# The end of a decoder trunk: sums of squares on TensorE, the last residual's place, and whole rows in the output transfers

## The chip, the cores and the metric

The kernel runs on one core of a Trainium2 chip. The metric is the device time of one execution in microseconds (us). The core has five engines that run side by side, each in its own instruction order: TensorE (PE, matrix products into PSUM), VectorE (DVE), ScalarE (ACT), GpSimd (POOL) and SyncE (SP), which issues most DMA transfers. They wait for one another through semaphores.

## The reference

One inference step of a trunk of two layers over 512 prompt tokens and 8 x 8 sample tokens, in float32, model width 1024. What matters here is the end: the feed-forward block of the second layer, its gated residual, and the final norm.

```python
D_MODEL = 1024; D_FF = 2816; EPS = 1e-6
def rms_norm(x, g):
    y = x * lax.rsqrt(jnp.mean(x * x, axis=-1, keepdims=True) + EPS)
    return y * g
def swiglu(h, w_in, w_out):
    gate, up = jnp.split(h @ w_in, 2, axis=-1)
    return (jax.nn.silu(gate) * up) @ w_out
def trunk(...):
    for l in range(DEPTH):
        ...   # layer 0: recurrent block; layer 1: sliding-window attention
        h = modulate(rms_norm(x, norm_g[l, 1]), sh2, sc2)
        x = x + g2[:, None, :] * swiglu(h, ffn_w_in[l], ffn_w_out[l])
        ...
    y = rms_norm(x, final_g)
```

## The kernel before

The tokens are worked on in two halves, h = 0 and h = 1, of 288 columns each: 256 prompt tokens and 32 sample tokens. The stream x[h] lies transposed in SBUF, as eight chunks c = 0 to 7 of 128 channels by 288 tokens; x_64 and x_65 are the two halves in the listings below. A float32 product is made of three float32r products of split operands, so a product of `K` blocks is 3 K matmuls of 128x288 columns (rows `mm<-sl,wh`).

The last stage of the feed-forward block (`out`, with the last group of hidden blocks) makes for each chunk m a product of 12 matmuls into a PSUM bank. `residual` then adds it to x: VectorE adds the prompt part (x<-mm,mods,x), makes the sample part in a buffer (ta<-mm,mods), and GpSimd adds it (x<-x,ta); for the very last chunk, 7, VectorE does that add too. `square` lets ScalarE square the finished chunk into a buffer ta and VectorE add it to the sum acc (acc_69 and acc_70 for the two halves); chunk 7 is not added there. `final_chunk` transposes the chunk on TensorE (mm<-ident,x: two of 128 columns and one of the 32 sample columns), and VectorE multiplies it by the gain into the output tiles (h<-mm,h; h_15729 in half 1): three tiles yt[h][0..2] of 128, 128 and 32 tokens by 1024 channels.

`final_norm`, when chunk 7 is done, squares it, sums over channels by products with a column of ones (mm<-small,acc and mm<-small,ta: the squares stand as weights, the ones are the moving column, one product for each of the three token groups in TOK), turns the sums into mean plus EPS on VectorE (tst<-mm), raises them to the power -1/2 on GpSimd (tst<-tst,small), scales the left 512 channels of each output tile on VectorE and the right 512 on ScalarE (h<-h,tst), and sends each half-tile to memory on SyncE's DMA queue.

Nothing of this is put on the engines as it is written. Every operation is recorded with an estimated cost, and a list scheduler (`schedule`) then fixes each engine's order; a recorded operation's priority is its place in the program, and `early(n)` moves everything inside it n places forward. In the trace every operation therefore has the one line of the recorder, L447, and is told apart by the names of its tiles.

Of the kernel before, what the change touches and what calls it, by code (L numbers as in the profile page):

```python
# [15 lines left out]
AF = mybir.ActivationFunctionType  # L16
ALU = mybir.AluOpType
AX = mybir.AxisListType

P = 128  # L20
D = 1024
KC = D // P
# [4 lines left out]
HP = 256  # L27
HC = 288
CW = 300
XW = 303  # L30
EPS = 1e-6
# [28 lines left out]
SH1, SC1, G1, SH2, SC2, G2 = range(6)  # L60
KVSH, KVSC = 6, 7
L1 = 8
# [411 lines left out]
def trunk_kernel(ctx, tc, a):  # L474
    nc = tc.nc
    rec = Recorder(a["shadow"])
    V, S, G, T, Q = (Engine(rec, n, o) for n, o in (("DVE", nc.vector), ("ACT", nc.scalar), ("POOL", nc.gpsimd), ("PE", nc.tensor), ("SP", nc.sync)))
# [5 lines left out]
    def const(shape, name, dt=F32):  # L483
        return cp.tile(shape, dt, tag=name, name=name)
# [3 lines left out]
    def ps(pool=pmm, tag="mm"):  # L488
        cnt[0] += 1
        return rec.tile(pool, tag, NMM if tag == "mm" else (8 - NMM), RMM if tag == "mm" else 1, [P, 512], F32, f"{tag}{cnt[0]}")  # L490

    def aux():
        return ps()

    x = [const([P, KC, HC], f"x{h}") for h in range(2)]
# [5 lines left out]
    ta = Slots(rec, cp, "ta", SLOT, NTA)  # L501
# [4 lines left out]
    ones, mhalf = small[:, 0:1], small[:, 4:8]  # L506
    mods = const([P, 14, KC, 9], "mods")
    acc = [const([P, HC], f"acc{h}") for h in range(2)]
    rstd = acc
    tst = [const([P, 6], f"tst{h}") for h in range(2)]  # L510
# [21 lines left out]
    @contextmanager  # L532
    def early(n):

        rec.bias -= n
        yield
        rec.bias += n
# [67 lines left out]
    pt = aux()  # L605
# [166 lines left out]
    def mp(g, c):  # L772
        return mods[:, g, c, 0:1]

    def msam(g, c, h):
        return mods[:, g, c, 1 + 4 * h : 5 + 4 * h].unsqueeze(2).to_broadcast([P, 4, NT])

    def v48(t):
        return t.rearrange("p (b t) -> p b t", b=4)


    def square(h, c):
        if c == 0:
            S.activation(acc[h][:], x[h][:, c, :], AF.Square)
        else:
            s = ta()
            S.activation(s.f[:, 0:HC], x[h][:, c, :], AF.Square)
            V.tensor_tensor(acc[h][:], acc[h][:], s.f[:, 0:HC], ALU.add)
            s.done()

    TOK = [slice(0, P), slice(P, 2 * P), slice(2 * P, HC)]

    def stats(h):
        pt = aux()
        st = tst[h][:, 0:3]
        for t, ts in enumerate(TOK):
            T.matmul(pt[0 : ts.stop - ts.start, t : t + 1], acc[h][:, ts], ones, start=True, stop=True)
# [4 lines left out]
    def spread(h, r0=0):  # L802
# [3 lines left out]
        o = aux()  # L806
        for t, ts in enumerate(TOK):
            r = slice(r0, r0 + 32) if t == 2 else ALL
# [152 lines left out]
    def drop(u):  # L961
        u.left -= 1
        if u.left == 0:
            u.hi.done()
            u.lo.done()
            nhi[0] -= 1
# [15 lines left out]
    def product(o, u, ops, first=True, last=True, col=0):  # L982
        n = u.kc * P // u.width
        hi, lo = u.hi.r, u.lo.r
        for k in range(n):
            xh, xl = ops[k]
            ks = slice(k * u.width + col, k * u.width + col + P)
            T.matmul(o, hi[:, ks], xh, start=(first and k == 0), stop=False)
            T.matmul(o, hi[:, ks], xl, start=False, stop=False)
            T.matmul(o, lo[:, ks], xh, start=False, stop=(last and k == n - 1))  # L990
# [17 lines left out]
    def residual(h, o, c, g, last):  # L1008
        xp, xs = x[h][:, c, 0:HP], v48(x[h][:, c, HP:HC])
        V.scalar_tensor_tensor(xp, o[:, 0:HP], mp(g, c), xp, ALU.mult, ALU.add)  # L1010
        t = ta()
        V.tensor_tensor(v48(t.f[:, 0:32]), v48(o[:, HP:HC]), msam(g, c, h), ALU.mult)
        (V if g == L1 + G2 and c == KC - 1 else G).tensor_tensor(xs, xs, v48(t.f[:, 0:32]), ALU.add)
        t.done()
        if last and (g != L1 + G2 or c < KC - 1):
            square(h, c)


# [123 lines left out]
    for i, w in enumerate(seq_):  # L1142
        c = int(w[1:])
# [4 lines left out]
        else:  # L1148
            first, last = ug[0] not in units, not any(v[0] == "g" for v in seq_[i + 1 :])
# [14 lines left out]
    for m in range(KC):  # L1164
# [3 lines left out]
            lambda h, o, m=m: residual(h, o, m, G1, True),  # L1168
# [8 lines left out]
    def ffn(l, g, after):  # L1177
# [18 lines left out]
        for f in range(PLAIN):  # L1196
            for w, ev in ((0, evac_gate), (1, evac_up(f))):
                c = 2 * f + w
# [78 lines left out]
        def pump(want=lambda: True):  # L1277
            while todo and (whs.live + todo[0][0] <= 2 * NHI):
                todo.popleft()[1]()
            assert want()  # L1280
            load_more()
# [69 lines left out]
        def out(k, m, h):  # L1351
            f0, us = outs[k]
            n, u = GROUPS[k], us[m]
            pump(lambda: u.hi is not None)
            o = ps()
            product(o[:, 0:HC], u, [(mid[h][f][0].r[:, 0:HC], mid[h][f][1].r[:, 0:HC]) for f in range(f0, f0 + n)], col=P * (m % 2) if u.width > P else 0)
            last = k == len(GROUPS) - 1
            residual(h, o, m, g, last)
            if last and l == 1:
                final_chunk(h, m)  # L1360
            drop(u)
            pump()
            if m == KC - 1:
                for f in range(f0, f0 + n):
                    for s_ in mid[h][f]:
                        s_.done()
                if last:
                    after(h)
# [404 lines left out]
    for w in ATT.split():  # L1773
        h, n = "AB".index(w[-1]), int(w[1:-1] or 0)
# [10 lines left out]
    yt = [None, None]  # L1785
# [14 lines left out]

    def final_norm(h):

        w = ta()
        S.activation(w.f[:, 0:HC], x[h][:, KC - 1, :], AF.Square)
        pt = [aux()[0 : ts.stop - ts.start, 0:1] for ts in TOK]
        st, rs = tst[h][:, 0:3], tst[h][:, 3:6]
        for i in range(2):
            for o, ts in zip(pt, TOK):
                T.matmul(o, (acc[h], w.f)[i][:, ts], ones, start=i == 0, stop=i == 1)
        w.done()  # L1810
        for t in range(3):
            n = P if t < 2 else 32
            V.tensor_scalar(st[0:n, t : t + 1], pt[t], 1.0 / D, EPS, ALU.mult, ALU.add)
            G.tensor_tensor(rs[0:n, t : t + 1], st[0:n, t : t + 1], mhalf[0:n, 0:1], ALU.pow)
            for i in range(2):
                cs = slice(512 * i, 512 * i + 512)
                y = yt[h][t][0:n, cs]
                if i:
                    S.activation(y, y, AF.Copy, scale=rs[0:n, t : t + 1])
                else:  # L1820
                    V.tensor_scalar(y, y, rs[0:n, t : t + 1], None, ALU.mult)
                if t < 2:
                    Q.dma_start(a["y_prompt"][0, h * HP + t * P : h * HP + (t + 1) * P, cs], y)
                else:
                    Q.dma_start(a["y_sample"][4 * h : 4 * h + 4].rearrange("b t d -> (b t) d")[:, cs], y)

    ffn1 = ffn(1, L1 + G2, final_norm)


# [172 lines left out]
```

## Time and profile before

| what | value |
|---|---|
| median of 3 runs | 1262.38 us (1261.91 to 1264.16) |
| profiled execution | 1263.01 us, its span 1261.2 us |
| TensorE busy | 1237.8 us, 98% of the span |
| VectorE, ScalarE, GpSimd busy | 920.3 us (73%), 663.1 us (53%), 252.7 us (20%) |
| share of the chain that ended last | TensorE 86%, VectorE 6%, ScalarE 4%, DMA 2% |
| output transfers of y | 8 of 256 KB, 4 of 64 KB |

The span runs from the first to the last instruction, and the execution's time lies 1.8 us above it. Busy shares are means over the whole span; the chain is followed back from the last instruction to what released it, step by step.

### The profile page before, as it was taken

The numbers are of one execution on the slowest core, as the hardware profiler recorded it, in microseconds if no ns is written. First come the engines' busy times: TensorE is split into PE (matmuls) and PEld (weight loads), VectorE is DVE, ScalarE is ACT, GpSimd is POOL, SyncE is SP. The second block draws the span as 40 slices with busy tenths as digits, with TensorE's granted clock in tenths as the row PEclk, the third lists the DMA queues.
The fourth block names the chain that finished last, engine by engine and source line by source line (L and its number), as shares of the span: only waits on it lengthen the run. The fifth ranks groups of instructions, "written<-read, shape, count | busy, mean of one in ns | idle before, by whom it ended". The sixth has DMA issues, their size and how long they took to land.

```text
span 1261.2 us, 25276 instructions
## 1 busy us (share of the span) xinstructions
PE 1237.8 (98%) x9532; PEld 1166.9 (93%) x9532; DVE 920.3 (73%) x2283; ACT 663.1 (53%) x1498; POOL 252.7 (20%) x542
## 2 busy tenths in 40 slices
PE   7999999999999999999999999999999999999997
PEld 5798999899899899989998997999999999999997
DVE  6998784795577468656778887558957865875776
ACT  4788973764255335514567678538523542552442
POOL 3456351101100010011024335100011011001011
PEclk8999999999999999999999999999999999999999
DMA  9955554535456655464513220332342232332322
GB/s 306 318 179 188 188 177 151 170 86 171 140 152 191 185 167 184 156 194 137 167 33 75 68 60 27 111 97 97 85 133 68 84 110 76 90 100 80 100 69 76
DMA packets 219755, 165.38 MB, mean 131 GB/s; under 512 B 23629, under 2 KB 204841, under 8 KB 219602
## 3 DMA queue, kind: packets, MB, share of 16 engines
q1 hardware_dynamic: 219186, 163.45, 43.0%
q8 instruction: 75, 1.23, 0.4%
q0 software_dynamic: 448, 0.32, 0.1%
q14 instruction: 46, 0.38, 0.1%
HBM read 160.85 MB, written 4.87 MB: 131 GB/s over the span
## 4 chain that ended last, share of the span: by engine, by line
PE 86%; DVE 6%; ACT 4%; DMA 2%; POOL 1%; issue 1%; SPq 0%; ACTq 0%; DVEq 0%
PE mm L447 82%; PE ada L447 4%; DVE wh L447 1%; DVE ta L447 1%; ACT tb L447 1%; DVE sl L447 1%; ACT ta L447 1%; DVE tb L447 1%; ACT h L447 1%; DMA raw<-in_rnn_w_in_dram 1%; ACT wh L447 1%; POOL h L447 1%; DMA reg<-in_ada_w_dram 1%; ACT sl L447 1%; DMA reg<-in_x_prompt_dram 1%
## 5 line engine op out<-in xcount | busy, mean ns | idle before, releaser
L447 PE MATMUL mm<-h,wh 128*128 128x288 f32 x4128 | 596.2, 298 | 3.8 <-ACT h L447 1.8
L447 PEld LDWEIGHTS mm<-h,wh 128*128 128x128 f32 x4128 | 560.5, 188 | 23.2 <-issue 11.3
L447 PE MATMUL mm<-sl,wh 128*128 128x288 f32 x3218 | 460.6, 296 | 0.4 <-ACT sl L447 0.3
L447 ACT CAST wh<-raw 128x512 fp32r<-128x512 f32 (+2 forms) x380 | 269.1, 721 | 345.7 <-PE mm L447 208.9
L447 PEld LDWEIGHTS mm<-sl,wh 128*128 128x128 f32 x3218 | 436.6, 188 | 9.0 <-issue 5.9
L447 DVE TENSOR_TENSOR wh<-raw,wh 128x512 fp32r<-128x512 f32 (+2 forms) x380 | 310.2, 828 | 59.3 <-ACT wh L447 57.0
L447 DVE SCALAR_TENSOR_TENSOR x<-mm,mods,x 128x256 f32<-128x256 f32 x160 | 77.0, 482 | 136.1 <-PE mm L447 136.0
L447 POOL TENSOR_TENSOR td<-td,td 128x288 f32<-128x288 f32 x38 | 35.5, 934 | 475.8 <-ACT td L447 467.7
L447 POOL TENSOR_TENSOR x<-x,ta 128x32 f32<-128x32 f32 x152 | 55.3, 364 | 331.1 <-DVE ta L447 325.9
L447 PE MATMUL mm<-tb,wh 128*128 128x288 f32 (+1 forms) x488 | 88.5, 296 | 0.4 <-ACT td L447 0.4
L447 PEld LDWEIGHTS mm<-tb,wh 128*128 128x128 f32 x488 | 72.4, 188 | 1.9 <-DVE sl L447 0.8
L447 ACT COPY td<-mm 128x288 f32<-128x288 f32 (+2 forms) x140 | 49.0, 364 | 37.7 <-DVE mm L447 18.0
L447 DVE TENSOR_TENSOR raw<-raw,raw 128x512 f32<-128x512 f32 x76 | 61.4, 808 | 0.9
L447 PE MATMUL mm<-ta,wh 128*128 128x288 f32 (+1 forms) x254 | 56.1, 298 | 0.0
L447 ACT ACTIVATE ta<-x 128x288 f32<-128x288 f32 x56 | 24.8, 444 | 55.6 <-POOL x L447 52.4
L447 DVE TENSOR_TENSOR raw<-raw 128x512 f32<-128x512 f32 x76 | 52.2, 688 | 1.1
L447 DVE TENSOR_TENSOR td<-mm,td 128x288 f32<-128x288 f32 x76 | 34.5, 454 | 23.4 <-PE mm L447 23.3
L447 PE MATMUL ada<-reg,cz 128*32 128x512 f32 (+1 forms) x448 | 49.5, 553 | 0.0
L447 PEld LDWEIGHTS mm<-ta,wh 128*128 128x128 f32 x254 | 41.7, 188 | 1.8 <-ACT wh L447 0.8
L447 ACT ACTIVATE ta<-ta,stat 128x128 f32<-128x128 f32 (+2 forms) x72 | 32.3, 471 | 18.5 <-DVE stat L447 17.7
L447 DVE TENSOR_TENSOR acc<-acc,ta 128x288 f32<-128x288 f32 x54 | 25.1, 464 | 12.4 <-ACT ta L447 12.4
L447 ACT CAST sl<-ta 128x288 fp32r<-128x288 f32 x54 | 23.0, 431 | 18.5 <-DVE ta L447 18.5
(202 smaller groups left out, 1197.9 us busy)
## 6 DMA issues: line engine op xcount, KB each, us to landing
raw<-in_ffn_w_in_dram SPq DMA_DIRECT2D x88, 512.0 KB
reg<-in_ada_w_dram SPq DMA_DIRECT2D x80, 512.0 KB
raw<-in_ffn_w_out_dram SPq DMA_DIRECT2D x48, 384.0 KB
raw<-in_rnn_w_in_dram SPq DMA_DIRECT2D x16, 512.0 KB
reg<-in_kv_ada_w_dram SPq DMA_DIRECT2D x16, 512.0 KB
wh<-in_ada_w_dram SPq DMA_DIRECT2D x24, 256.0 KB
raw<-in_rnn_w_out_dram SPq DMA_DIRECT2D x8, 512.0 KB
raw<-in_ffn_w_out_dram SPq DMA_DIRECT2D x8, 512.0 KB
```

Source lines behind the costliest of these rows:

```text
L447: self.rec.add(eng, lambda: getattr(obj, name)(*map(real, args), **{k: real(v) for k, v in kw.items()}), cost, outs, ins, func, lat, port, ...
```

## The change

The change has three parts. The square of chunk 6 is no longer added to acc on VectorE: it is kept in its buffer (`late_square`) and summed by three more products with ones, into the same PSUM column as acc and the square of chunk 7. All products with ones of a half now go to one PSUM bank, in three columns, so that one VectorE instruction makes the statistic of both 128-token groups and the powers are two GpSimd instructions of one and two columns instead of three. The residual of chunk 7 and the sums are recorded 60 places earlier. And each output tile is sent in one transfer of rows of 1024 channels, instead of two of 512.

```diff
         V.tensor_tensor(v48(t.f[:, 0:32]), v48(o[:, HP:HC]), msam(g, c, h), ALU.mult)
         (V if g == L1 + G2 and c == KC - 1 else G).tensor_tensor(xs, xs, v48(t.f[:, 0:32]), ALU.add)
         t.done()
-        if last and (g != L1 + G2 or c < KC - 1):
+        if last and g == L1 + G2 and c == KC - 2:
+            late_square[h] = s = ta()
+            S.activation(s.f[:, 0:HC], x[h][:, c, :], AF.Square)
+        elif last and (g != L1 + G2 or c < KC - 1):
             square(h, c)
...
-            residual(h, o, m, g, last)
+            with early(60 if last and l == 1 and m == KC - 1 else 0):
+                residual(h, o, m, g, last)
...
-        w = ta()
-        S.activation(w.f[:, 0:HC], x[h][:, KC - 1, :], AF.Square)
-        pt = [aux()[0 : ts.stop - ts.start, 0:1] for ts in TOK]
-        st, rs = tst[h][:, 0:3], tst[h][:, 3:6]
-        for i in range(2):
-            for o, ts in zip(pt, TOK):
-                T.matmul(o, (acc[h], w.f)[i][:, ts], ones, start=i == 0, stop=i == 1)
-        w.done()
+        with early(60):
+            w = ta()
+            S.activation(w.f[:, 0:HC], x[h][:, KC - 1, :], AF.Square)
+            pt = aux()
+            st, rs = tst[h][:, 0:3], tst[h][:, 3:6]
+            sums = (acc[h], late_square[h].f, w.f)
+            for i, y in enumerate(sums):
+                for t, ts in enumerate(TOK):
+                    T.matmul(pt[0 : ts.stop - ts.start, t : t + 1], y[:, ts], ones, start=i + t == 0, stop=i == 2, skip_group_check=True)
+            late_square[h].done()
+            w.done()
+            V.tensor_scalar(st[:, 0:2], pt[:, 0:2], 1.0 / D, EPS, ALU.mult, ALU.add)
+            G.tensor_tensor(rs[:, 0:1], st[:, 0:1], mhalf[:, 0:1], ALU.pow)
+            V.tensor_scalar(st[0:32, 2:3], pt[0:32, 2:3], 1.0 / D, EPS, ALU.mult, ALU.add)
+            G.tensor_tensor(rs[:, 1:3], st[:, 1:3], mhalf[:, 1:3], ALU.pow)
         for t in range(3):
             n = P if t < 2 else 32
-            V.tensor_scalar(st[0:n, t : t + 1], pt[t], 1.0 / D, EPS, ALU.mult, ALU.add)
-            G.tensor_tensor(rs[0:n, t : t + 1], st[0:n, t : t + 1], mhalf[0:n, 0:1], ALU.pow)
             for i in range(2):
-                cs = slice(512 * i, 512 * i + 512)
-                y = yt[h][t][0:n, cs]
+                y = yt[h][t][0:n, 512 * i : 512 * i + 512]
                 if i:
                     S.activation(y, y, AF.Copy, scale=rs[0:n, t : t + 1])
                 else:
                     V.tensor_scalar(y, y, rs[0:n, t : t + 1], None, ALU.mult)
-                if t < 2:
-                    Q.dma_start(a["y_prompt"][0, h * HP + t * P : h * HP + (t + 1) * P, cs], y)
-                else:
-                    Q.dma_start(a["y_sample"][4 * h : 4 * h + 4].rearrange("b t d -> (b t) d")[:, cs], y)
+            y = yt[h][t][0:n, :]
+            if t < 2:
+                Q.dma_start(a["y_prompt"][0, h * HP + t * P : h * HP + (t + 1) * P, :], y)
+            else:
+                Q.dma_start(a["y_sample"][4 * h : 4 * h + 4].rearrange("b t d -> (b t) d"), y)
```

What the scheduler makes of it is seen in three places. TensorE at the end of half 1, before: the last matmul of the last product (mm_16161), then the transposes of chunk 6 (mm_16181) and chunk 7 (mm_16192) and the products with ones.

```order
L447 MATMUL mm_16161<-sl_15749,wh_15717 128x288
L447 MATMUL mm_16181<-ident,x_65 128x128 [waits DVE_49]
L447 MATMUL mm_16181<-ident,x_65 128x128
L447 MATMUL mm_16181<-ident,x_65 32x128 [waits Pool_49]
L447 MATMUL mm_16192<-ident,x_65 128x128 [waits DVE_49]
L447 MATMUL mm_16192<-ident,x_65 128x128
L447 MATMUL mm_16198<-small,acc_70 128x1 [waits DVE_49,PE_49]
L447 MATMUL mm_16201<-small,acc_70 128x1
L447 MATMUL mm_16205<-small,acc_70 32x1 [waits PE_49]
L447 MATMUL mm_16192<-ident,x_65 32x128 [waits DVE_49]
L447 MATMUL mm_16198<-small,ta_16203 128x1 [waits Activation_49]
```

The same place after: the last product is mm_16153, the transposes of chunk 6 are mm_16168, and ta_16175 is the late square.

```order
L447 MATMUL mm_16168<-ident,x_65 128x128 [waits DVE_49]
L447 MATMUL mm_16168<-ident,x_65 128x128
L447 MATMUL mm_16153<-sl_15649,wh_15701 128x288
L447 MATMUL mm_16153<-sl_15661,wh_15701 128x288
L447 MATMUL mm_16177<-small,acc_70 128x1 [waits DVE_49]
L447 MATMUL mm_16177<-small,acc_70 128x1
L447 MATMUL mm_16177<-small,acc_70 32x1
L447 MATMUL mm_16177<-small,ta_16175 128x1 [waits Activation_49]
L447 MATMUL mm_16177<-small,ta_16175 128x1
L447 MATMUL mm_16177<-small,ta_16175 32x1
L447 MATMUL mm_16168<-ident,x_65 32x128 [waits Pool_49]
L447 MATMUL mm_16153<-sl_15649,wh_15717 128x288
```

The transposes of chunk 6 and six products with ones now stand inside the last product, which ends with four matmuls behind them (the first is the last row shown); behind it come the transposes of chunk 7 and the three products with ones of its square.

VectorE in the same stretch, before, from the last product's residual on.

```order
L447 SCALAR_TENSOR_TENSOR x_65<-mm_16161,mods,x_65 128x256 [waits PE_49]
L447 TENSOR_TENSOR ta_16189<-mm_16161,mods 128x32 [waits Pool_49]
L447 TENSOR_TENSOR h_15729<-mm_16181,h_15729 128x128 [waits PE_49]
L447 TENSOR_TENSOR acc_70<-acc_70,ta_16186 128x288 [waits Activation_49]
L447 TENSOR_TENSOR h_15729<-mm_16181,h_15729 128x128
L447 TENSOR_TENSOR h_15729<-mm_16181,h_15729 32x128
L447 TENSOR_TENSOR x_65<-x_65,ta_16189 128x32 [waits DVE_49]
```

After, from the output products of chunk 6 on.

```order
L447 TENSOR_TENSOR h_15729<-mm_16168,h_15729 128x128 [waits PE_49]
L447 TENSOR_TENSOR h_15729<-mm_16168,h_15729 128x128
L447 TENSOR_TENSOR h_15729<-mm_16168,h_15729 32x128
L447 SCALAR_TENSOR_TENSOR x_65<-mm_16153,mods,x_65 128x256 [waits PE_49]
L447 TENSOR_TENSOR ta_16194<-mm_16153,mods 128x32
L447 TENSOR_TENSOR x_65<-x_65,ta_16194 128x32 [waits DVE_49]
```

The add of squares is gone, the output products of chunk 6 stand ahead of the last residual, and its three instructions follow one another.

SyncE's queue at its end, after: the three output tiles of half 0 (h_15697, the two prompt tiles in one row) and the three of half 1. Before, each half had six rows of 512 columns here, each waiting for one engine's half-tile.

```order
L447 DMA out_y_prompt_dram<-h_15697 128x1024 [waits DVE_49,Activation_49] x2
L447 DMA out_y_sample_dram<-h_15697 32x1024 [waits DMAHW5_49,DVE_49,Activation_49]
L447 DMA out_y_prompt_dram<-h_15729 128x1024 [waits DMAHW6_49,DVE_49,Activation_49]
L447 DMA out_y_prompt_dram<-h_15729 128x1024 [waits DMAHW7_49,DVE_49,Activation_49]
L447 DMA out_y_sample_dram<-h_15729 32x1024 [waits DMAHW0_49,DVE_49,Activation_49]
```

Each transfer now waits for VectorE and ScalarE both.

More of the change, by code (lines that the diff above doesn't have):

```diff
@@ L789, in square @@
             s.done()
+    late_square = [None, None]
     TOK = [slice(0, P), slice(P, 2 * P), slice(2 * P, HC)]
```

## The prediction

> **What bounds the kernel now.** I read the page first: TensorE is busy for 98% of the span, so anything put into its stream ahead of the last product is paid for unless it lies in a gap. Then I read the chain of waits of the last 82 us. It runs on TensorE alone until 1251.18 us and then through a tail of 10 us in which no product is left.
>
> ```profile
> 1179.96 71.22 PE mm L447 x545
> ...
> 1251.20 0.48 DVE x L447
> ...
> 1254.29 0.56 POOL tst L447
> ...
> 1254.88 1.33 ACT h L447 x2
> 1256.21 0.61 ACTq L1998
> ```
>
> Next came the timelines of the single engines. VectorE's rows of the tail (start, length, operation, idle time ahead of it) show that between the last residual (x<-mm,mods,x) and the last add of samples (x<-x,ta, 1252.66) lie an accumulation of squares and the output products of chunk 6 (h<-mm,h). The first two rows are the same pair of operations in the first half, where nothing lies between.
>
> ```profile
> 1235.90 0.17 DVE L447 TENSOR_TENSOR ta<-mm,mods 128x32 f32<-128x32 f32 x1
> 1236.10 0.19 DVE L447 TENSOR_TENSOR x<-x,ta 128x32 f32<-128x32 f32 x1
> ...
> 1251.20 0.48 DVE L447 SCALAR_TENSOR_TENSOR x<-mm,mods,x 128x256 f32<-128x256 f32 x1 [0.27 <-PE mm L447]
> 1251.60 0.18 DVE L447 TENSOR_TENSOR ta<-mm,mods 128x32 f32<-128x32 f32 x1
> 1251.70 0.28 DVE L447 TENSOR_TENSOR h<-mm,h 128x128 f32<-128x128 f32 x1
> 1251.90 0.45 DVE L447 TENSOR_TENSOR acc<-acc,ta 128x288 f32<-128x288 f32 x1
> 1252.26 0.47 DVE L447 TENSOR_TENSOR h<-mm,h 128x128 f32<-128x128 f32 x2
> 1252.66 0.17 DVE L447 TENSOR_TENSOR x<-x,ta 128x32 f32<-128x32 f32 x1
> 1253.48 0.67 DVE L447 TENSOR_TENSOR h<-mm,h 128x128 f32<-128x128 f32 x3 [0.65 <-PE mm L447]
> 1254.08 0.28 DVE L447 TENSOR_SCALAR tst<-mm 128x1 f32<-128x1 f32 x3
> 1254.88 1.58 DVE L447 TENSOR_SCALAR h<-h,tst 128x512 f32<-128x512 f32 x3 [0.51 <-POOL tst L447]
> ```
>
> TensorE's rows, at the end of the first half and at the very end. A product with ones (mm<-small) is two instructions in the trace.
>
> ```profile
> 1235.27 0.38 PE L447 MATMUL mm<-sl,wh 128*128 128x288 f32 x1
> 1235.48 0.56 PE L447 MATMUL mm<-small,acc 128*128 128x1 f32 x4
> 1235.91 0.51 PE L447 MATMUL mm<-sl,wh 128*128 128x288 f32 x2
> 1236.35 0.22 PE L447 MATMUL mm<-small,acc 128*32 128x1 f32 x2
> 1236.50 0.40 PE L447 MATMUL mm<-sl,wh 128*128 128x288 f32 x1
> 1236.74 0.27 PE L447 MATMUL mm<-ident,x 128*32 128x128 f32 x1
> 1236.76 0.64 PE L447 MATMUL mm<-sl,wh 128*128 128x288 f32 x3
> 1237.24 0.65 PE L447 MATMUL mm<-small,ta 128*128 128x1 f32 x6
> 1237.82 0.93 PE L447 MATMUL mm<-sl,wh 128*128 128x288 f32 x5
> 1238.59 0.38 PE L447 MATMUL mm<-ident,x 128*128 128x128 f32 x2
> ...
> 1249.20 1.96 PE L447 MATMUL mm<-sl,wh 128*128 128x288 f32 x13
> 1251.00 1.18 PE L447 MATMUL mm<-ident,x 128*128 128x128 f32 x5
> 1252.49 0.73 PE L447 MATMUL mm<-small,acc 128*128 128x1 f32 x6 [0.32 <-DVE acc L447]
> 1253.15 0.28 PE L447 MATMUL mm<-ident,x 128*32 128x128 f32 x1
> 1253.42 0.76 PE L447 MATMUL mm<-small,ta 128*128 128x1 f32 x6
> ```
>
> ScalarE, GpSimd and the DMA queue of SyncE at the end, then the outputs' transfers in slices of 0.2 us (last two numbers: share of the DMA engines, GB/s).
>
> ```profile
> 1252.92 0.44 ACT L447 ACTIVATE ta<-x 128x288 f32<-128x288 f32 x1 [1.19 <-DVE x L447]
> 1254.88 1.95 ACT L447 ACTIVATE h<-h,tst 128x512 f32<-128x512 f32 x3 [1.51 <-POOL tst L447]
> 1255.39 0.35 SPq L447 DMA_DIRECT2D out_y_prompt_dram<-h  x1
> 1257.30 1.16 SPq L447 DMA_DIRECT2D out_y_sample_dram<-h  x2
> 1256.20:1256.40 0.20, 0.00 (x0) 0.00 (x0) 0.20 (x1) 0.20 (x2) 0.00 (x0) 0.50 0.73 266
> 1258.40:1258.60 0.20, 0.00 (x0) 0.00 (x0) 0.00 (x0) 0.00 (x0) 0.00 (x0) 0.50 1.00 379
> 1259.40:1259.60 0.20, 0.00 (x0) 0.00 (x0) 0.00 (x0) 0.00 (x0) 0.00 (x0) 0.50 0.63 154
> ```
>
> The engines are full from 1256.2 to about 1259.5: once begun, the six transfers end when their bytes are through, and the span ends 1.7 us later, at 1261.2.
>
> **The change part by part.**
>
> *Products with ones.* Each half gains three (the square of chunk 6 goes through them instead of the VectorE add). In half 1 the order also moves all six for acc and chunk 6, and the three transposes of chunk 6, from behind the last product to inside it; the products are the same. The matmul step is (1251.00 - 1249.20) / 13 = 0.138 us. A set of three products with ones takes 1237.82 - 1237.24 = 0.58, and the five matmuls behind it 0.77 instead of 0.69, so 0.66 with the switch back. The split set of the first half costs more: from 1235.27 to 1237.24 there are 1.97 us with seven matmuls (0.97) and a 32-row transpose; 0.9 is left. From 1237.82 to 1251.00 there are 84 matmuls (11.59) and six sets of transposes: 1.59 / 6 = 0.26 a set.
>
> First half: three unbroken sets, 3 x 0.66 = 1.98, against 0.9 + 0.66 = 1.56: +0.42. Second half, ahead of the end of the last product: 2 x 0.66 + 0.26 = +1.58. TensorE shows no idle time in this stretch, so the last product ends 2.0 us later. Bounds: 0, if they fell into gaps; 3.2, if every set cost the 0.9 of the split one (3 x 0.9 - 1.56 + 2 x 0.9 + 0.26). I take 2.0, from the unbroken set, because the order now shows unbroken sets.
>
> [...]
>
> *Waits this adds.* The ones of the late square wait for ScalarE; behind them on TensorE stand a transpose and the last four matmuls. Behind the wait of a scaling on GpSimd in half 0 stands the residual's sample part of half 1's chunk 0, which TensorE needs only ten matmuls (1.4 us) into a later product. I cost both at nothing, and come back to them as a rival. The DMA of the first half's outputs is covered by more than 10 us of products.
>
> *The residual ahead.* In the order the last residual still stands behind the three output products of chunk 6. They start 1253.48 - 1253.15 = 0.33 after their last transpose and hold VectorE for 0.60, together 0.93; that transpose stands four matmuls from the end, and those end for VectorE after 4 x 0.138 + (1251.20 - 1251.00) = 0.75. So the residual starts 0.18 late: +0.15 with rounding. Bounds 0 and 0.6.
>
> *From the residual to the first scaling.* Before: 1254.88 - 1251.20 = 3.68. After, from the residual's start: ta at 0.40, the add 0.20 behind it at 0.60 (as at 1236.10) and over at 0.79; square 0.09 later (1252.83 to 1252.92), over at 1.32; ones at 1.38, over at 2.14; the 128x2 statistic at 2.18, 0.13 long (now it waits for all three products); GpSimd 0.08 later, 0.56 long, to 2.95; scaling at 2.98. Gain 0.70: the add of samples comes 0.86 earlier, since the add of squares (0.36) and the output products of chunk 6 (0.20 + 0.40) no longer stand ahead of it, and 0.16 goes back to the wait for all three ones. The output products of chunk 7, 1.19 to 1.86 by the same steps, are done before the ones. Bounds of the gain 0.5 and 0.9.
>
> *Output.* The second power now has two columns; 128x1 takes 0.56 and nothing in the tail has two, so between 0.56 and twice that; it is wanted 0.62 after the first scaling and starts 0.5 ahead of it, so at 0.6 it is on time and at 1.1 it delays tile 1 alone, behind 1.4 us of tile 0's bytes. A transfer of a whole tile must wait for ScalarE's half. Two of ScalarE's scalings take 1.33 us (the chain) and three 1.95, so the step is 0.62 and the first ends 0.71 behind its start; with 0.05 to the issue that is 0.76, instead of 1255.39 - 1254.88 = 0.51 for VectorE's half: +0.25. Three issues fewer gain nothing, since the bytes, 288 rows of 4 KB, are the same and fill the engines without a gap. Rows of 4 KB instead of 2 KB are in no store of this trace; if the last 0.6 us ran at 379 GB/s, 0.2 would be saved, and 0.2 the other way is as far as I go.
>
> Sum: +2.0 + 0.15 - 0.70 + 0.25 = **+1.7 us**. The profiled execution took 1263.01 us for a span of 1261.2; 1264.7 on it. The median of the runs, 1262.38, lies 0.63 below that execution, so I predict **1264.1**, 0.13% more. A measurement of this kernel can tell about 0.2%, 2.5 us, from no change: the forecast is no change that can be told.
>
> **The rivals.**
> *TensorE waits for the late squares (slower).* For: the path from a residual to the end of its square crosses VectorE, GpSimd and ScalarE (in the tail 1251.20 to 1253.36 with other work between), and behind the wait stands the last product. Against: in half 1 the order leaves TensorE eight matmuls, a set of transposes and the acc set first, 8 x 0.138 + 0.26 + 0.66 = 2.0 us. It decides from a path longer than that. The one such wait of the trace lasts 0.32 (at 1252.49); at three places 1.0 us: +2.7, 1265.1. 13%.
> *The added TensorE work is hidden.* If the two halves' sets filled gaps, the sum is 0.15 - 0.70 + 0.25 = -0.3: 1262.1. Against: 98% busy, and 0.08 us of switch visible behind a set. 10%.
> *Fewer transfers are worth their fixed cost (faster).* If SyncE's issues paced the output, the end would follow the last issue: about 1257.9 now, 3.0 behind the scaling, and 2.1 after (three tile steps of ScalarE): -0.9 instead of +0.25, sum +0.5, 1262.9. Against: 1.00 share at 379 GB/s with no gap. 4%; and 4% for a gain above 2.5 us from what no row here shows. [...]
>
> **How the numbers follow.** Forecast 69%, slower rival 13%, hidden 10%, transfers 4% + 4%. The forecast's own range is 1262.8 to 1265.6: the matmul term halfway to its bounds, 1.0 and 2.6, with 0.15 - 0.70 + 0.25 the sum is 0.7 to 2.3, and the other bounds widen it by 0.3 below and 0.9 above. The range 1261.9 to 1265.8 takes in the hidden case and the slower rival too. Faster 0.04, slower 0.13 (that rival, part of it below 2.5 us, and the forecast's own upper edge), same 0.83.
>
> **What would show it.** Right: the last product's matmuls end about 2 us later in the span; from the last residual to the first scaling 3.0 us; the first output issue 0.75 behind the scaling; three transfers filling the engines for 3.3 us. Wrong: idle time of TensorE ahead of a product with ones from ta, more than 0.3 us of it; an end of the span less than 5.9 us behind the scaling, which would give the transfers a price; a set of ones below 0.4 us in the stream.

## The result and the profile after

| | median of 11 runs | range | profiled execution | its span |
|---|---|---|---|---|
| before | 1262.49 us | 1261.91 to 1265.12 | 1263.01 us | 1261.2 us |
| after | 1266.22 us | 1263.42 to 1266.96 | 1266.39 us | 1264.3 us |

The ratio is 1.002, with a 95% interval of 1.0011 to 1.0029: the changed kernel is slower by 1.4 to 3.7 us. That is at the edge of what can be told here; the median lies 2.1 us above the forecast and 0.4 above its range. The two medians stand 3.7 us apart, but the means of the same runs, 1263.19 and 1265.58, only 2.4. A repeat (below) gave 1265.02 us and 1.0017 (1.0006 to 1.0027).

To compare profiles I cut the end of the span at three rows that every kernel of this study has: a 32-row transpose in the first half (the marker), the start of the last residual's x<-mm,mods,x on VectorE, and the start of the first scaling h<-h,tst. Stretch A runs from the marker to the residual, B from there to the scaling, C from there to the end of the span. The marker, on TensorE before and after (start, length, operation):

```profile
1230.89 0.27 PE L447 MATMUL mm<-ident,x 128*32 128x128 f32 x1
```

```profile
1231.77 0.27 PE L447 MATMUL mm<-ident,x 128*32 128x128 f32 x1
```

Up to here both kernels issue the same instructions, and the second profile is already 0.9 us later. That part of the 3.1 us between the spans isn't the change's (the last section shows what goes with it). The rest is A 20.31 to 22.54, B 3.67 to 3.38, C 6.36 to 6.57: +2.23, -0.29 and +0.21.

The chain of waits after (start, length, what):

```profile
1179.97 73.71 PE mm L447 x569
...
1253.70 0.67 DVE h L447 x3
1254.38 0.39 DVE x L447
...
1254.90 0.20 DVE x L447
...
1255.12 0.45 ACT ta L447
...
1255.62 1.22 PE mm L447 x6
...
1256.86 0.22 DVE tst L447 x2
...
1257.10 0.57 POOL tst L447
...
1257.69 1.39 ACT h L447 x2
1259.08 0.61 ACTq L2009
```

TensorE's run on the chain ends 2.5 us later than before, and the path behind it is the one that the order shows: output products of chunk 6, the three residual instructions, the square, the last products with ones, one statistic, one power, two scalings of ScalarE. TensorE's timeline after:

```profile
1252.11 0.66 PE L447 MATMUL mm<-small,acc 128*128 128x1 f32 x6
1252.69 0.76 PE L447 MATMUL mm<-small,ta 128*128 128x1 f32 x6
1253.38 0.28 PE L447 MATMUL mm<-ident,x 128*32 128x128 f32 x1
1253.42 0.77 PE L447 MATMUL mm<-sl,wh 128*128 128x288 f32 x4
1254.82 0.68 PE L447 MATMUL mm<-ident,x 128*128 128x128 f32 x3 [0.63 <-DVE x L447]
1255.62 1.21 PE L447 MATMUL mm<-small,ta 128*128 128x1 f32 x6
```

The two sets of products with ones stand inside the last product without idle time ahead of them: 0.58 for the first, 0.69 to the transpose for the second. But the last set, which is on the chain, takes 1.21 us where the same six instructions took 0.76 before. VectorE after:

```profile
1253.70 0.67 DVE L447 TENSOR_TENSOR h<-mm,h 128x128 f32<-128x128 f32 x3 [1.25 <-PE mm L447]
1254.31 0.46 DVE L447 SCALAR_TENSOR_TENSOR x<-mm,mods,x 128x256 f32<-128x256 f32 x1
1254.70 0.17 DVE L447 TENSOR_TENSOR ta<-mm,mods 128x32 f32<-128x32 f32 x1
1254.90 0.19 DVE L447 TENSOR_TENSOR x<-x,ta 128x32 f32<-128x32 f32 x1
1255.54 0.68 DVE L447 TENSOR_TENSOR h<-mm,h 128x128 f32<-128x128 f32 x3 [0.45 <-PE mm L447]
1256.86 0.21 DVE L447 TENSOR_SCALAR tst<-mm 128x2 f32<-128x2 f32 x2 [0.64 <-PE mm L447]
1257.69 0.49 DVE L447 TENSOR_SCALAR h<-h,tst 128x512 f32<-128x512 f32 x1 [0.62 <-POOL tst L447]
```

The add of samples comes 0.59 behind the residual instead of 1.46. Behind the output products of chunk 7, VectorE then waits 0.64 for the slow products with ones. What goes with their 1.21 us is the granted clock, 0.50 during that set in the second row below. (A row of this view has the stretch and its length, the busy time and number of instructions of TensorE, its weight loads, VectorE, ScalarE and GpSimd, then the granted clock, the share of the DMA engines, and GB/s.)

```profile
1254.10:1255.20 1.10, 0.47 (x4) 0.26 (x3) 0.96 (x5) 0.08 (x1) 0.00 (x0) 1.00 0.00 0
1255.60:1257.00 1.40, 1.21 (x6) 1.10 (x6) 0.76 (x5) 0.00 (x0) 0.00 (x0) 0.50 0.00 0
```

At 1255.22 TensorE's clock fell from 1.00 to 0.50 for the rest of the span, 0.91 us behind the last residual's start. Before, it fell 4.98 us behind it, when all products were done. Last, SyncE's queue and the transfers after:

```profile
1258.44 1.00 SPq L447 DMA_DIRECT2D out_y_prompt_dram<-h  x2
1259.72 0.38 SPq L447 DMA_DIRECT2D out_y_sample_dram<-h  x1
```

```profile
1260.00:1260.20 0.20, 0.00 (x0) 0.00 (x0) 0.00 (x0) 0.00 (x0) 0.00 (x0) 0.50 1.01 410
1262.20:1262.40 0.20, 0.00 (x0) 0.00 (x0) 0.00 (x0) 0.00 (x0) 0.00 (x0) 0.50 0.88 246
1262.40:1262.60 0.20, 0.00 (x0) 0.00 (x0) 0.00 (x0) 0.00 (x0) 0.00 (x0) 0.50 0.04 0
```

The first issue is 0.75 behind the scaling instead of 0.51, and three transfers fill the engines until about 1262.5, 1.7 us ahead of the end.

### The profile page after: what moved, and what is told of

Its sections match the earlier page's. It is cut to its first block, busy times and chain, and to the rows that moved or that the text cites. A ratio compares the mean times of both kernels' runs of the same rounds, so it can differ in the third digit from the quotient of the medians.

```text
span 1264.3 us, 25286 instructions
## 1 busy us (share of the span) xinstructions
PE 1241.3 (98%) x9544; PEld 1170.5 (93%) x9544; DVE 919.7 (73%) x2279; ACT 663.3 (52%) x1498; POOL 253.3 (20%) x540
## 3 DMA queue, kind: packets, MB, share of 16 engines
HBM read 160.85 MB, written 4.87 MB: 131 GB/s over the span
## 4 chain that ended last, share of the span: by engine, by line
PE 87%; DVE 4%; ACT 4%; DMA 2%; issue 1%; POOL 1%; SPq 1%; ACTq 0%; DVEq 0%
PE mm L447 83%; PE ada L447 4%; DMA reg<-in_x_prompt_dram 1%; DVE wh L447 1%; ACT ta L447 1%; ACT tb L447 1%; SPq L447 1%; DVE ta L447 1%; ACT h L447 1%; DVE sl L447 1%; DVE tb L447 1%; ACT sl L447 1%; DMA reg<-in_ada_w_dram 0%; ACT wh L447 0%; ACT L447 0%
```

## The experiments

Stretches in us; "fall" is how long behind the last residual's start the clock fell to half for the rest of the span. "Outside" is what the profiled execution took beyond its span.

| kernel | A | B | C | sum | fall | outside | median (runs) | ratio to before (95%) |
|---|---|---|---|---|---|---|---|---|
| before | 20.31 | 3.67 | 6.36 | 30.35 | 4.98 | 1.8 | 1262.49 (11) | |
| before, again | 20.32 | 3.67 | 6.35 | 30.34 | 3.33 | 1.8 | 1261.64 (1) | |
| after | 22.54 | 3.38 | 6.57 | 32.49 | 0.91 | 2.1 | 1266.22 (11) | 1.002 (1.0011 to 1.0029) |
| after, first repeat | 22.52 | 3.39 | 6.54 | 32.46 | 1.02 | 2.1 | 1265.02 (10) | 1.0017 (1.0006 to 1.0027) |
| after, second repeat | 22.54 | 3.40 | 6.57 | 32.51 | 0.71 | 2.1 | 1264.88 (1) | |
| after, third repeat | 22.54 | 2.95 | 6.55 | 32.04 | 2.21 | 2.1 | 1263.40 (1) | |
| whole rows only | 20.54 | 3.48 | 7.27 | 31.30 | 4.34 | 1.8 | 1263.86 (10) | 1.001 (1.0 to 1.0021) |
| ones held behind | 21.18 | 3.06 | 6.57 | 30.81 | 5.25 | 2.1 | 1264.13 (10) | 1.0014 (1.0004 to 1.0025) |
| no early | 21.18 | 3.08 | 6.55 | 30.82 | 3.85 | 2.1 | 1263.91 (10) | 1.0008 (0.9998 to 1.0018) |
| half rows | 22.54 | 2.94 | 6.15 | 31.63 | 2.54 | 2.1 | 1264.39 (1) | |
| mixed | 20.43 | 3.06 | 6.29 | 29.78 | 5.53 | 1.8 | 1262.88 (11) | 1.0001 (0.9992 to 1.001) |
| residual early only | 20.35 | 3.02 | 6.84 | 30.21 | 4.98 | 1.8 | 1262.62 (11) | 0.9999 (0.999 to 1.0008) |
| late square in half 1 only | 21.78 | 2.94 | 6.57 | 31.29 | 2.80 | 1.8 | 1263.33 (10) | 1.0003 (0.9994 to 1.0013) |
| one set more | 23.23 | 3.19 | 6.56 | 32.97 | 1.58 | 2.1 | 1266.53 (1) | |

My theory was that of the forecast: every set of ones in TensorE's stream ahead of the end of the last product costs its time. The rivals were that part of it is hidden or comes from elsewhere; and for the 0.4 us missing in B there were two causes to tell apart, the clock and the one PSUM bank (the statistic now waits for all three products).

**The changed kernel again** (no edit).

> The changed kernel unaltered, once more. Three stretches are compared in every run: A, from the 32-row transpose that stands 20 us ahead of the last residual (1230.89 us in the profile before, 1231.77 in the one after; the orders are the same up to it) to the start of the last residual on VectorE; B, from there to the first scaling of the output; C, from there to the end of the span. Before they were 20.31, 3.68 and 6.32 us, after 22.54, 3.38 and 6.61. Theory 1: B is 3.0 us by its own steps, and 0.4 more was the TensorE clock, which fell to 0.50 at 1255.2 us, ahead of the last three products with ones, and falls at a time that has nothing to do with the program; so A and C repeat within 0.1, and B is either about 3.0 or about 3.4, 3.0 where the clock falls later than those products. Theory 2: the wait for all three products in one bank costs the 0.4; B is 3.4 whenever the clock falls.

The stretches repeat to 0.03 us, with the clock's fall 1.02 us behind the residual. A second repeat:

> The changed kernel unaltered, a third profile. Two of two so far had the clock at half speed from 0.91 and 1.02 us behind the last residual, ahead of the last set of ones (1.21 us long instead of 0.76). Theory 1, the fall has a phase of its own: sooner or later a profile has it elsewhere, with that set at 0.7 to 0.76 and B at 2.9 to 3.0. Theory 2, the stretch of ones and idle time inside the last product brings the fall on at the same place each time: B 3.4 again, with the fall 0.9 to 1.1 us behind the residual.

Again the same stretches. Three profiles of three showed the early fall, so it looked like a property of the program.

**Whole rows only**: the kernel before, with the three output transfers of whole tiles.

```diff
-                if t < 2:
-                    Q.dma_start(a["y_prompt"][0, ..., cs], y)
...
+            y = yt[h][t][0:n, :]
+            if t < 2:
+                Q.dma_start(a["y_prompt"][0, ..., :], y)
...
```

> The kernel before with only the output transfers changed to whole rows of 1024 channels, one per tile. Theory 1: the bytes pace the output and the first issue waits for ScalarE's half, so C grows from 6.32 to 6.6 us. Rival, fewer transfers save a fixed cost each: C falls to 5.2 us or less. A and B stay within 0.3 us of 20.31 and 3.68, whatever the scheduler reorders.

C was 7.27 us, 0.9 more than before, where the changed kernel with the same transfers has 6.57. The windows show what goes with it:

```profile
1257.60:1257.80 0.20, 0.00 (x0) 0.00 (x0) 0.00 (x0) 0.00 (x0) 0.00 (x0) 0.50 1.25 471
1259.00:1259.20 0.20, 0.00 (x0) 0.00 (x0) 0.00 (x0) 0.00 (x0) 0.00 (x0) 0.50 0.05 20
```

An 8 KB fetch of instructions (the trace's queue of that kind) ran at 1257.61 in the middle of the transfers, and a few last packets then trickled until 1259.2 instead of ending with the rest. In the kernel before and in the changed kernel that fetch comes behind the end of the span (at 1261.60 against 1261.2, and at 1265.88 against 1264.3). No run moves the fetch alone, so that it is the cause is not shown; but this run does not price whole rows. (A and B moved too, by +0.23 and -0.19: with the transfers changed, the scheduler put two of chunk 6's transposes inside the last product.)

**The sets of ones held behind the last product**: the changed kernel, in which the products with ones for acc and the late square of half 1 wait for the last product.

```diff
...
+                rec.hold = [last_o[h]] if h == 1 and i < 2 else []
...
```

> The changed kernel, but in half 1 the products with ones of acc and of the late square may not be scheduled ahead of the last product's end; nothing else is altered. Theory 1, the place in TensorE's stream is what costs: A falls from 22.54 by the two sets, 1.3 us, to 21.2, while B stays at 3.0 to 3.5, because TensorE is idle there anyway. Rival, the wait of the late square for ScalarE or the moved residual costs it: A stays above 22.2.

A fell by 1.36 us, to 21.18. TensorE's timeline shows both sets behind the last matmuls, and the last set in 0.70 with the clock still at 1.00:

```profile
1252.54 0.64 PE L447 MATMUL mm<-sl,wh 128*128 128x288 f32 x3
1253.02 0.65 PE L447 MATMUL mm<-small,acc 128*128 128x1 f32 x6
1253.61 0.76 PE L447 MATMUL mm<-small,ta 128*128 128x1 f32 x6
1254.30 0.55 PE L447 MATMUL mm<-ident,x 128*128 128x128 f32 x3
1254.68 0.70 PE L447 MATMUL mm<-small,ta 128*128 128x1 f32 x6
```

Behind the product the sets run in the time in which VectorE and ScalarE work on the residual and its square, and cost nearly nothing here: B is 3.06, where the changed kernel has 3.38 to 3.40 with the early fall and 2.95 without.

**No early**: the changed kernel with both moves of 60 places taken out.

```diff
-            with early(60 if last and l == 1 and m == KC - 1 else 0):
+            with early(0):
...
-        with early(60):
+        with early(0):
```

> The changed kernel without both moves of 60 places (the residual of chunk 7 and the sums are recorded where they stand). The order then has the products with ones of half 1 behind the last product, and the output products of chunk 6 still ahead of the last residual. Theory 1: A 21.2 us, as with the sets held behind; B 3.0 to 3.4; C 6.6; the whole 1.0 to 1.4 us below the changed kernel. Rival, the move is what shortens B: B goes back to 3.6.

The same stretches as with the hold, to 0.02 us. It is the early move that puts the two sets inside the last product, and it buys next to nothing in B.

**Half rows**: the changed kernel with the six half-tile transfers of before.

```diff
-            y = yt[h][t][0:n, :]
-            if t < 2:
-                Q.dma_start(a["y_prompt"][0, ..., :], y)
+                if t < 2:
+                    Q.dma_start(a["y_prompt"][0, ..., cs], y)
...
```

> The changed kernel with the output sent in half-tiles of 512 columns again, as before; the rest is unaltered. The rows-only run gave C 7.27 us, above the 6.57 of the changed kernel, but its last packets came from one straggling stretch (174 GB/s from 1258.2 us), so the size of this part is still open. Theory 1, the first issue waits for ScalarE's half: the first issue comes 0.5 us behind the scaling instead of 0.75, C falls from 6.55 to 6.3 to 6.4, A stays 22.5. Rival, fewer and larger transfers are worth something: C rises above 6.6.

C was 6.15, less than the 6.3 to 6.4 expected and 0.4 us below the changed kernel. But the last byte is through 4.81 us behind the scaling, against 4.87 with whole rows. The rest of the 0.4 lies between the last byte and the end of the span: 1.34 us here, 1.70 in the changed kernel, and 1.56 in the kernel before, which has the same six transfers as this run. What sets that last piece is not shown. SyncE issued the first transfer 0.52 behind the scaling (at 1256.10):

```profile
1256.62 1.81 SPq L447 DMA_DIRECT2D out_y_prompt_dram<-h  x4
1258.52 1.16 SPq L447 DMA_DIRECT2D out_y_sample_dram<-h  x2
```

B was 2.94, with the one PSUM bank as in the changed kernel and the clock's fall 2.54 us behind the residual. The wait for all three products in one bank is therefore not what kept B at 3.38.

**Mixed**: late square in half 1 only, its sets held behind the last product, tile 0 in half rows, tiles 1 and 2 in whole rows.

```diff
-            sums = (acc[h], late_square[h].f, w.f)
+            sums = (acc[h], late_square[h].f, w.f) if h else (acc[h], w.f)
...
+                rec.hold = [last_o[h]] if h == 1 and i < 2 else []
...
+                if t == 0:
+                    Q.dma_start(a["y_prompt"][0, h * HP : h * HP + P, cs], y)
...
```

> A version put together from the runs so far: the square of chunk 6 is taken out of the VectorE sum in half 1 alone; in half 1 the products with ones of acc and of the late square are held behind the last product; output tile 0 goes in two half-tiles, tiles 1 and 2 in whole rows. Theory 1: A 20.3 to 20.5 us (0.66 to 0.85 below the 21.18 of the run with the sets held behind), B 3.1, C 6.2, together 29.7, which is 0.65 below the 30.35 of the kernel before; the runs' ratio cannot tell that from 1 for sure. Rival, the moved sets are not what A pays for: A stays at 21.2 and the whole above 30.35.

The sum is 29.78, 0.57 below before, but a ratio of 1.0001 (0.9992 to 1.001) cannot tell that from nothing.

**The residual early only**: the kernel before, with the residual of chunk 7 recorded 60 places earlier.

```diff
-            residual(h, o, m, g, last)
+            with early(60 if last and l == 1 and m == KC - 1 else 0):
+                residual(h, o, m, g, last)
```

> The kernel before with one edit: the residual of chunk 7 is recorded 60 places earlier; squares, products with ones and transfers as before. In its order the three steps of the last residual then stand ahead of the output products of chunk 6, with one add of squares between. Theory 1: the shorter way from the residual to the scaling needs no more products with ones; A 20.3 to 20.5, B 3.1 to 3.3, C 6.35, together 29.8 to 30.1, 0.3 to 0.5 below before. Rival, the gain in B comes from taking the add of squares away: B stays at 3.6.

B fell from 3.67 to 3.02 with no product more, and A stayed. VectorE now has the add of samples behind the add of squares but ahead of the output products:

```profile
1250.53 0.48 DVE L447 SCALAR_TENSOR_TENSOR x<-mm,mods,x 128x256 f32<-128x256 f32 x1 [0.39 <-PE mm L447]
1250.92 0.18 DVE L447 TENSOR_TENSOR ta<-mm,mods 128x32 f32<-128x32 f32 x1
1251.02 0.45 DVE L447 TENSOR_TENSOR acc<-acc,ta 128x288 f32<-128x288 f32 x1
1251.39 0.18 DVE L447 TENSOR_TENSOR x<-x,ta 128x32 f32<-128x32 f32 x1
...
1253.55 1.58 DVE L447 TENSOR_SCALAR h<-h,tst 128x512 f32<-128x512 f32 x3 [0.30 <-POOL tst L447]
```

C took 6.84 instead of the 6.35 expected: the 8 KB fetch of instructions again fell into the transfers (over at 1257.60), and 0.48 of the 0.65 was given back. Ratio 0.9999: no change that can be told.

**The late square in half 1 only**: the changed kernel, the first half summed as before.

```diff
-        if last and g == L1 + G2 and c == KC - 2:
+        if last and g == L1 + G2 and c == KC - 2 and h == 1:
...
-            sums = (acc[h], late_square[h].f, w.f)
+            sums = (acc[h], late_square[h].f, w.f) if h else (acc[h], w.f)
...
```

> The changed kernel with the late square in the second half alone (the first half adds the square of chunk 6 on VectorE as before and has two sets of products with ones). Theory 1 (each set in TensorE's stream costs its own time): from the marker transpose to the last residual 22.54 less one set and its split, 0.42 to 0.75, so 21.8 to 22.1; if the clock falls as in the changed kernel, 3.39 to the first scaling, otherwise 2.95; to the end 6.55. Rival (the first half's third set is covered by its gaps): 22.5 from the marker to the residual. On the time outside the span: 1.8 us if it goes with the length of the program, 2.1 if it goes with the transfers of whole tiles.

A was 21.78, 0.76 less than in the changed kernel. That is the first half's third set together with a new order: the two sets that are left there stand side by side, which they do neither before (where the first is split) nor after (where matmuls of a product stand between all three).

```profile
1234.87 0.70 PE L447 MATMUL mm<-small,acc 128*128 128x1 f32 x6
1235.50 0.76 PE L447 MATMUL mm<-small,ta 128*128 128x1 f32 x6
```

B was 2.94, the fall coming 2.80 behind the residual. Outside the span it took 1.8 us with whole-tile transfers, so the 2.1 does not go with those.

**One set more**: three products with ones of the late square into a bank that nobody reads, in half 1.

```diff
+            if h == 1:
+                extra = aux()
+                for t, ts in enumerate(TOK):
+                    T.matmul(extra[0 : ts.stop - ts.start, t : t + 1], late_square[h].f[:, ts], ones, start=t == 0, stop=t == 2, skip_group_check=True)
```

> The changed kernel with one set of three products with ones more (of the late square, in a bank of its own that nobody reads) inside the last product of the second half. Theory 1 (a set costs its 0.66 us wherever it stands ahead of the end of the last product): from the marker transpose to the last residual 22.54 + 0.66 = 23.2 us, the rest as in the changed kernel (3.4 and 6.55 with an early fall of the clock, 2.95 without). Rival (one set lies in a gap of TensorE's stream and costs nothing): 22.5.

A rose by 0.69, to 23.23. TensorE runs twelve instructions from ta in a row:

```profile
1252.34 1.45 PE L447 MATMUL mm<-small,ta 128*128 128x1 f32 x12
```

The clock fell 1.58 behind the residual, in the middle of the last set, and B is between the two other values: 3.19.

**Both kernels once more**, to tell whether the early fall belongs to the program.

> The changed kernel, unchanged, a fourth profile. Theory 1 (the early fall belongs to the program): from the marker transpose to the last residual 22.5 us, to the first scaling 3.39, to the end 6.55, 32.5 in all; the clock falls 0.7 to 1.1 us behind the last residual's start and the last set of products with ones takes 1.21 us; the execution is 2.1 us longer than its span. Theory 2 (chance): the fall comes 2.5 us or more behind the residual, the set takes 0.76 and the stretch to the first scaling 2.95.

> The kernel before, unchanged, once more, as the counterpart of the repeats of the changed kernel. Theory 1 (the early fall of TensorE's clock belongs to the changed program): from the 32-row transpose of chunk 4 in half 1 to the last residual 20.3 us, from there to the first scaling 3.65, to the end 6.4, 30.3 in all; the clock falls for good 4 to 5 us behind the last residual's start, not 1 us; the execution is 1.8 us longer than its span. Theory 2 (the fall is a matter of chance in any program): it may fall about 1 us behind the residual here too, and the last set of products with ones then takes 1.2 us instead of 0.76.

(The marker is the same row of the first half throughout, also where the text says half 1.) The kernel before repeated its stretches to 0.01 us. In the changed kernel's fourth profile the clock fell 2.21 behind the residual, just behind the last set of ones. TensorE's and VectorE's rows, and the clock during that set:

```profile
1253.09 0.76 PE L447 MATMUL mm<-small,ta 128*128 128x1 f32 x6 [0.19 <-ACT ta L447]
```

```profile
1251.77 0.46 DVE L447 SCALAR_TENSOR_TENSOR x<-mm,mods,x 128x256 f32<-128x256 f32 x1
...
1254.71 0.48 DVE L447 TENSOR_SCALAR h<-h,tst 128x512 f32<-128x512 f32 x1 [0.62 <-POOL tst L447]
```

```profile
1253.00:1253.90 0.90, 0.76 (x6) 0.66 (x6) 0.62 (x4) 0.03 (x1) 0.00 (x0) 1.00 0.00 0
```

B is 2.94 between these rows: the forecast's 2.98. So the same program has B 2.95 or 3.39, by where the clock's fall lies. "Three of three" had been too few to call it the program's.

## Why the prediction was right or wrong

*Products with ones and transposes (forecast +2.0, with the late residual +2.15; measured A +2.23).* Right in size and part by part. The residual starts 0.12 behind the end of the last matmuls (1254.31 against 1253.42 + 0.77) where it was 0.04 before (1251.20 against 1249.20 + 1.96): +0.08, forecast +0.15. The two sets inside the last product and this 0.08 together cost 1.36 (22.54 - 21.18, and 21.78 - 20.43 = 1.35 without the first half's third set), so the sets 1.28; the forecast had 2 x 0.66 = 1.32. One more set costs 0.69.

The first half's third set is not the 0.76 of the run without it, since that run has another order. It is read from the rows. A set after takes 0.59 to the next matmul of the product, and the eight matmuls behind it 1.16 instead of 8 x 0.132 (the median step between two matmuls in the trace): 0.69 with this switch back, 2.1 for the three.

```profile
1235.90 0.66 PE L447 MATMUL mm<-small,ta 128*128 128x1 f32 x6
1236.49 1.33 PE L447 MATMUL mm<-sl,wh 128*128 128x288 f32 x8
1237.65 0.49 PE L447 MATMUL mm<-ident,x 128*128 128x128 f32 x3
```

Before, by the same count, the split set took about 0.8 and the other 0.69, so the first half pays about +0.6, where the forecast had +0.42. About 0.3 is left for the three transposes of chunk 6 (2.23 - 1.36 - 0.6), forecast 0.26. The forecast's matmul step of 0.138 holds a switch; with 0.132 its own 13.18 us leave 0.35 for a set of transposes. The misses are small, and no large ones had to cancel.

*From the residual to the scaling (forecast -0.70; measured -0.72 once, -0.28 three times).* The mechanism was right: the add of samples came 0.87 earlier (0.59 instead of 1.46), and 2.95 is the forecast's 2.98. What the step missed is TensorE's clock: its last products with ones, from 1.38 to 2.14 behind the residual, are priced at the 0.76 us that they took at a clock of 1.00. With the sets of ones and the transposes of chunk 6 moved ahead of it, TensorE has less to do behind the last product and idles 0.63 us. In three of the four profiles the clock fell while the last set of ones was still to come, and the set then took 1.21 instead of 0.76.

*Output (forecast +0.25; measured +0.2).* The wait for ScalarE's half was right: the first issue comes 0.75 behind the scaling. The trace's packets give the parts: first byte 1.60 behind the scaling instead of 1.36 (+0.24), all bytes through in 3.27 instead of 3.44 us (-0.17), the end 1.70 behind the last byte instead of 1.56 (+0.14). The last two, which the sum had at nothing, cancel; that is luck.

*Outside the span (not in the forecast; measured +0.35).* See the last section.

By profile the sum is +2.23 - 0.28 + 0.21 + 0.35 = 2.5 us with the early fall and 2.1 without, against the forecast's 1.7. The repeat measured 1265.02 - 1262.46 = 2.56. The first comparison's medians stand 3.73 apart, 1.2 more, but that is where its runs happen to lie: five of the changed kernel's eleven took 1263.4 to 1265.3 at granted clocks of 0.994 to 0.996, six took 1266.2 to 1267.0 at 0.990 to 0.992, and the median is the lowest of the six. The means of the same runs are 2.39 apart, those of the repeat 2.36, and both agree with the profiles. So the forecast was short by 0.4 us outside the span and, where the clock fell early, by another 0.4 in the tail. (The lower end of the forecast's range widens the sum by 0.3, where the bounds that it names add up to 0.15 + 0.2 + 0.2 = 0.55; no measured time lies there.)

*The rivals.* TensorE did not wait for late squares: no idle time stands ahead of the sets inside the product. The added work is not hidden: A moves by 0.64 to 0.69 for each set taken out of the last product or put into it. Fewer transfers earned nothing: six half-tile transfers ended in 6.15 us, three whole ones in 6.55.

## What to carry to other kernels

On this TensorE, busy for 98% of the span, moving small products from behind the last large product to inside it cost their whole time, while behind it they ran beside the tail of the other engines: 1.36 us of the 2.2, and the kernel without the early moves had all of the same gain but 0.13 us. A cheap reordering of the engine that is really late (the residual alone, 0.65 us of B in its profile) needs none of the work that was added for it. And a chain that ends on a small TensorE operation should be priced at both clocks that the traces show, since the same program ran its last set in 1.21 us at 0.50 and in 0.76 at 1.00.

## What the hardware showed that was not expected

**The clock's fall in the tail.** The same program meets the clock's fall at other places in other executions: in the four profiles of the changed kernel the last one lies 0.91, 1.02, 0.71 and 2.21 us behind the residual's start. In the seven profiles of kernels with the sets inside the last product (after four times, half rows, half 1 only, one set more) it lies 0.71 to 2.80 us behind; in the seven others (before twice, whole rows, held behind, no early, mixed, residual early) 3.33 to 5.53. The groups do not overlap, and only in the first did it ever come ahead of the end of the last set of ones (four of seven). The shortest stretch at half clock in the profiles of before and after took 3.41 us (from 787.59 in the latter). In the 3.41 us ahead of the last fall, TensorE's rows were busy for 2.78 us in the profile after, 2.46 in its third repeat, 0.31 with the sets held behind and 1.41 before. In the 3.41 us ahead of those it was 3.41 after, 3.41 with the sets held behind and 2.95 before. So in these three the fall came behind a stretch in which TensorE had less to do than just before; that less work brings it on is not shown. In the profile before, the 3.41 us from 689.57 had TensorE's rows busy for 2.39 us, less than those 2.78, and the clock was 1.00 in the 3.41 us behind them. And the kernels differ in more than the work behind the last product, so that part is not shown alone. The 3.41 us ahead of the fall in the profile after:

```profile
1251.81:1255.22 3.41, 2.78 (x24) 2.37 (x22) 1.99 (x10) 0.54 (x2) 0.16 (x1) 1.00 0.00 0
```

TensorE's rows are busy for 2.78 of it, 1.3 of that with products of one column.

**Half clock in the middle of the program.** The 0.9 us by which the second profile was late at the marker go with two stretches at a clock of 0.50. Near the start it spent 10.24 us at it (from 19.59) where the profile before spent 6.83 (from 20.56), and it had one more such stretch, of 3.41 us, at 787.6. Ahead of the first, the same matmul started 0.8 us earlier than in the profile before (14.04 against 14.87), behind it 0.5 later (35.31 against 34.81); ahead of the second it was 0.6 late (787.48 against 786.87), behind it 1.3 (791.82 against 790.51). After and before there:

```profile
787.60:791.00 3.40, 3.40 (x14) 2.59 (x15) 2.94 (x16) 3.02 (x8) 1.15 (x2) 0.50 0.69 202
```

```profile
787.60:791.00 3.40, 2.96 (x21) 2.19 (x19) 3.33 (x19) 3.18 (x8) 1.15 (x2) 1.00 0.74 214
```

TensorE's rows fill that stretch in the profile after, but not the one ahead of it: in the 3.41 us before 787.59 they were busy for 2.98 us, with products of 64 to 256 columns. How much of an execution runs at half clock changes with the execution: over the span the changed kernel had a mean granted clock of 0.991 in this profile and 0.996 in its third repeat, and the marker lies at 1231.8 in the first and at 1229.2 in the second. A difference of 1 us between two spans says nothing until it is cut at a common row.

**Rows of 4 KB and of 2 KB.** A packet of 4 KB took 164 ns (median of 288) and one of 2 KB 87 ns (of 576), and the 1.18 MB were through in 3.27 us in whole rows, in 3.44 in half rows.

**0.35 us outside the span.** The six profiles of programs with 25,267 to 25,278 instructions took 1.8 us beyond their span, the eight with 25,284 to 25,299 took 2.1. Neither the transfers (half rows: 2.1) nor the early moves (no early: 2.1) decide it. All eight also sum a late square in the first half, which none of the six does, so the length of the program is not shown alone. Nor is it fixed for a program: the ten runs of no early took 1.82 to 2.14 beyond theirs. What happens in that time no trace shows.
